# A two-block transformer stack on one core: one matmul of 512 columns for the high weights, and token-major blocks of 512

## The chip, the cores and the metric

The kernel runs on one core of a Trainium2 chip. The time is that of the device, in microseconds, of one execution of the whole program; less is better.

## The reference

Two blocks of two layers each work on 256 tokens of 1024 features, in float32. Cut to what matters here:

```
def first_block(...):                                # two layers
    h = h + 0.5 * swiglu(rms_norm(h, g1), w_in, w_out)        # 1024 -> 2 x 2816 -> 1024
    u = rms_norm(h, g); split(u @ w_in)                        # 11312 columns
    merged = sigmoid(gate_s) * (mamba2(...) @ w_s) + sigmoid(gate_d) * (deltanet(...) @ w_d)
    h = h + merged @ w_out
    h = h + 0.5 * swiglu(rms_norm(h, g2), w_in2, w_out2)
def second_block(...):                               # two layers
    u = rms_norm(h, g); q, k, v, g_ret, c_in, gates = split(u @ w_in)   # 10240 columns
    y_a = (silu(g_ret) * group_norm(chunk_retention(rot(q), rot(k), v))) @ w_ret_out
    y_b = silu(layer_norm(dwconv31(a * sigmoid(b)))) @ w_conv_out + bias
    h = h + (g_a * y_a + g_b * y_b) @ w_mix_out
    h = h + cross_attention(rms_norm(h), rms_norm(mem)) @ w_xo
    h = h + (silu(dwconv3(gate)) * val) @ w_down               # 1024 -> 2 x 2816 -> 1024
```

Almost all of the arithmetic is in the weight products.

## The kernel before

The residual stream `h` lies in SBUF as four tiles of 128 features x (2 feature tiles x 256 tokens). All weights are streamed once from HBM, in parts of [128 x 1024] (512 KB), 938 of them. `wpart` (L182) loads a part by DMA into `wr`, ScalarE casts it to `wh` (fp32r, the high part, L187), VectorE subtracts to get `wl` (the low part, L189). Each of these has four buffers. The activations are split in the same way, into tiles of high parts and tiles of low parts (class `X`, L192), each tile with two feature tiles of 256 tokens side by side. A product is then three matmuls of 256 columns: high weights by high x, high weights by low x, low weights by high x.

`proj_fm` (L202) makes two tiles of 128 output features in one PSUM bank `pw`: for each of the two and for each 128 rows of the contraction it issues the three matmuls, with the weights stationary and 256 tokens moving:

```
TE.matmul(o, a, x.h(k), start=(k == 0), stop=False)
TE.matmul(o, a, x.l(k), start=False, stop=False)
TE.matmul(o, b, x.h(k), start=False, stop=(k == KT - 1))
```

With a contraction of 1024 such a unit takes two weight parts and 48 matmuls. `proj_tm` (L219) makes the products that are wanted with tokens on partitions (`zd`, `zs`, `v`, `g` and the values of the cross attention): x is stationary there and 256 columns of the weights move, again three matmuls, for two token tiles, in one bank.

`ffn` (L331) and `conv_ffn` (L1103) loop over eleven pairs of a gate and an up unit, and then call `out_proj` (L326), four units with a contraction of 2816. In front of the product x carries the gain of the norm only; the reciprocal root mean square (`rb`) is multiplied in where the accumulator is evacuated, since it is not ready when the stream begins. `mixer1` (L399) holds the delta rule and the state space branch, `mixer2` (L830) the retention (`rot` L914, `by_tokens` L922) and the convolution branch of 31 taps (L902), `xattn` (L1048) the cross attention.

What sets the order: the stream has the highest priority (`AHEAD`), and `tick()` (L161) lets the other work, written as generators ("chains"), go one step after each part of a unit; the convolution's taps are dealt out by `PUMP` = 3.1 per part, each behind the subtraction that was issued last. A scheduler places instructions on each engine by these priorities. PSUM has eight banks: four single-bank buffers of `pw` for the stream, four of `pm` for everything else.

Of the kernel before, what the change touches and what calls it, by code (L numbers as in the profile page):

```python
# [15 lines left out]
P = 128  # L16
# [8 lines left out]
AHEAD = 100000  # priority of what the weight stream needs  # L25
PUMP = 3.1  # convolution taps dealt out per unit of the weight stream

# per-feature vectors, one column of 128 features each: name -> columns per layer
# [25 lines left out]
# column ranges of w_in, in the order in which they are streamed  # L54
# [15 lines left out]
W1F, W1T = _starts(W1_FM, 128), _starts(W1_TM, 256)  # L70
W2F, W2T = _starts(W2_FM, 128), _starts(W2_TM, 256)


def _kernel(tc, t):
    nc = tc.nc
    V, A, G, TE = nc.vector, nc.scalar, nc.gpsimd, nc.tensor
    with ExitStack() as es:
# [22 lines left out]

        def pw():
            return pwp.tile([P, 512], F32, name="pw")
# [51 lines left out]
        def split(hi, lo, src):  # L154
            A.copy(hi, src)
            sub(lo, src, hi.bitcast(F32))

# [34 lines left out]
        class X:  # L192
            def __init__(self):
                self.hi, self.lo = [], []

            def h(self, k):
                return self.hi[k // 2][:, (k % 2) * 256:(k % 2) * 256 + 256]

            def l(self, k):
                return self.lo[k // 2][:, (k % 2) * 256:(k % 2) * 256 + 256]  # L200

        def proj_fm(w, i, KT, x):  # L202
            """tiles i, i+1 of w (features on partitions): one bank [128, (2, 256 tokens)]"""
            p = pw()
            for m in range(2):
                o = p[:, m * 256:m * 256 + 256]
                for k0 in range(0, KT, 8):
                    kt = min(8, KT - k0)
                    hi, lo = wpart(w[i + m, :, k0 * 128:(k0 + kt) * 128], kt * 128)
                    for kk in range(kt):  # L210
                        k = k0 + kk
                        a, b = hi[:, kk * 128:kk * 128 + 128], lo[:, kk * 128:kk * 128 + 128]
                        TE.matmul(o, a, x.h(k), start=(k == 0), stop=False)  # L213
                        TE.matmul(o, a, x.l(k), start=False, stop=False)  # L214
                        TE.matmul(o, b, x.h(k), start=False, stop=(k == KT - 1))  # L215
                    tick()
            return p

        def proj_tm(w, i, x):  # L219
            """block i (256 columns) of w, tokens on partitions: one bank [128, (2 token tiles, 256)]"""  # L220
            parts = [wpart(w[i, :, q * 1024:(q + 1) * 1024], 1024) for q in range(2)]
            p = pw()
            for tk in range(2):
                o = p[:, tk * 256:tk * 256 + 256]
                s = slice(tk * 128, tk * 128 + 128)
                for k in range(8):
                    hi, lo = parts[k // 4]
                    a, b = hi[:, (k % 4) * 256:(k % 4) * 256 + 256], lo[:, (k % 4) * 256:(k % 4) * 256 + 256]
                    TE.matmul(o, x.h(k)[:, s], a, start=(k == 0), stop=False)  # L229
                    TE.matmul(o, x.l(k)[:, s], a, start=False, stop=False)  # L230
                    TE.matmul(o, x.h(k)[:, s], b, start=False, stop=(k == 7))  # L231
                tick()
            return p

# [1 line left out]
        class Norm:  # L236
            def __init__(self, g, alloc=None):
                self.g, self.x, self.acc = g, X(), None
                self.alloc = alloc
# [5 lines left out]
            def operand(self, j, h):  # L245
                if self.alloc is None:
                    hi = xp.tile([P, 512], F32R, name="xh")
                    lo = xp.tile([P, 512], F32R, name="xl")
                else:
                    hi, lo = self.alloc(F32R), self.alloc(F32R)  # L250
                for m in range(2):
                    k = 2 * j + m
                    s = slice(m * 256, m * 256 + 256)
                    A.activation(hi[:, s], h[:, s], AF.Copy, scale=self.g[:, k:k + 1])
                    V.scalar_tensor_tensor(lo[:, s], h[:, s], self.g[:, k:k + 1], hi[:, s].bitcast(F32), op0=ALU.mult, op1=ALU.subtract)
                self.x.hi.append(hi)
                self.x.lo.append(lo)
# [8 lines left out]
            def scaled(self, h):  # L266
                """the normalized operand itself"""
                y = X()
                for j in range(4):
# [4 lines left out]
                    hi, lo = xp.tile([P, 512], F32R, name="xh"), xp.tile([P, 512], F32R, name="xl")  # L274
                    split(hi, lo, v)
                    y.hi.append(hi)
                    y.lo.append(lo)
# [18 lines left out]
        def total(acc):  # L296
            """sums over features of a tile of feature pairs: a bank's [128 tokens, 2 token tiles]"""
# [6 lines left out]
        def rows(col, name):  # L304
            """[128 tokens, 2] -> [128, 256 tokens], the same on each partition"""
# [25 lines left out]
        def ffn(h, L, nrm, w1, w2, nxt):  # L331
# [3 lines left out]
            for j in range(NF // 2):  # L335
                pg = proj_fm(w1[L], 2 * j, 8, x)
                pu = proj_fm(w1[L], NF + 2 * j, 8, x)
                g, u = cv(), cv()
                mul(r2(g), r2(pg), rbb)
                A.activation(g, g, AF.Silu)  # L340
                mul(r2(u), r2(pu), rbb)
                mul(g, g, u)
                hi, lo = sa(F32R), sa(F32R)
                split(hi, lo, g)
                hid.hi.append(hi)
                hid.lo.append(lo)

            def evac(j, p):
                V.scalar_tensor_tensor(h[j], p, 0.5, h[j], op0=ALU.mult, op1=ALU.add)
# [4 lines left out]
        def conv_silu(p, rb, w, K, nt, c0, bias, dst):  # L354
            """causal depthwise convolution of two tiles (p times rb, or p alone), then silu"""
# [18 lines left out]
        def fm(tiles, i, c):  # L374
            """feature tile i, chunk (or token tile) c"""
# [8 lines left out]
        def to_features(tm, u, g, dst):  # L384
            """two feature tiles 2u, 2u+1 of tm (by tokens), times the gains g, as hi and lo"""
# [4 lines left out]
            hi, lo = sa(F32R), sa(F32R)  # L390
            n = 512 // g.shape[1]
            for m in range(g.shape[1]):
                s = slice(m * n, m * n + n)
                A.activation(hi[:, s], p[:, s], AF.Copy, scale=g[:, m:m + 1])
                V.scalar_tensor_tensor(lo[:, s], p[:, s], g[:, m:m + 1], hi[:, s].bitcast(F32), op0=ALU.mult, op1=ALU.subtract)
            dst.hi.append(hi)
            dst.lo.append(lo)

        def mixer1(h, L, nrm, nxt):  # L399
# [4 lines left out]
            # small projections: dt (32), a (8), b (8)  # L404
# [18 lines left out]
            # softplus(x) = max(x, 0) + log1p(exp(-|x|)), log1p(e) = 2 atanh(e / (2 + e))  # L423
# [18 lines left out]
            # cumulated decays: by column (tokens on partitions), totals, by row (through DRAM)  # L442
# [16 lines left out]
            def fetch(r0, c):  # L459
                """rows r0..r0+3 of the cumulated decays, chunk c, on each partition"""  # L460
# [5 lines left out]
            def decays(dst, r0, c):  # L466
                """fetched rows to exp(min(row - column, 0)): [column token, (4, row token)]"""
# [5 lines left out]
            # -- gated delta rule, four heads at a time: chunks of 128, unnormalized k and q, their norms folded into the scalings --  # L473
# [7 lines left out]
            def ssq(tiles):  # L481
                """rsqrt of the sums of squares over features: columns (chunk, head)"""
# [14 lines left out]
            def delta(hh, kf, qf, vf, zd):  # L497
# [6 lines left out]
                # M[i, j] = c1[i] exp(G_i - G_j) k_i k_j (its lower part counts); a[j, i] = exp(G_i - G_j) q_i k_j for j <= i  # L504
# [21 lines left out]
                # Y = transposed inverse of I + M, by doubling the diagonal blocks; Z = its transpose (32-column windows)  # L526
# [15 lines left out]
                def aside():  # L542
                    """what the inverse does not need: k by tokens, scaled for the state (chunk 0) and for w (chunk 1); a; v; scales of q"""
# [14 lines left out]
                for lvl in range(1, 6):  # L558
                    # rows of the upper blocks: (off-diagonal block of the transposed M) times Y, then Y times that
# [114 lines left out]
            def tm_silu(dst, i, u):  # L674
                p = proj_tm(wt, i + u, state1["x"])
# [637 lines left out]
```

## Time and profile before

| | us |
|---|---|
| median of 3 runs | 2968.93 |
| lowest and highest run | 2967.71, 2970.07 |
| span of the profiled execution (first to last instruction) | 2968.0 |
| TensorE busy | 2950.8 (99%) |
| VectorE busy | 2202.5 (74%) |
| ScalarE busy | 1526.6 (51%) |

The time of the profiled execution is its span and the little that lies around it; the three runs are within 0.1% of each other. Busy times are sums of records of an engine; the records of matmuls overlap, so a busy TensorE says that it always had one under way. Where an engine was idle, the views name what ended the idle time. A window is a stretch of the span, counted from its first instruction.

### The profile page before, as it was taken

To read this page: it belongs to the slowest core of one execution; us is meant where nothing else is said; L and a number is where in the kernel's file an instruction comes from. 1 tells how busy PE (TensorE), PEld (TensorE's weight loads), DVE (VectorE), ACT (ScalarE), POOL (GpSimd) and SP (SyncE) were. 2 spreads that over 40 slices of the span, in tenths; PEclk is the share of its full clock that TensorE was granted. 3 is DMA by queue.
4 is the path that set the end of the run, shared out by engine and by line. 5 is a ranking of instruction groups with operands and counts; after the bars stand their busy time and mean duration, and the time that the engine had idled before them with its cause. 6 is when DMAs were issued, how large, how long until landed. Compare 5 with 4: busy or idle time off the path is not lost.

```text
span 2968.0 us, 62381 instructions
## 1 busy us (share of the span) xinstructions
PE 2950.8 (99%) x26256; PEld 2911.2 (98%) x26256; DVE 2202.5 (74%) x3498; ACT 1526.6 (51%) x2080; POOL 95.0 (3%) x113
## 2 busy tenths in 40 slices
PE   8999999999999999999999999999999999999998
PEld 8999999999999999999999999999999999999998
DVE  6658878866666578788665799976676899876774
ACT  5446456544444465465454544545554444554553
POOL 0000001100000001011000000000000000000000
PEclk9999999999999999999999999999999999999999
DMA  6555444455655555444556555555456554554554
GB/s 229 180 172 185 144 136 136 161 181 185 180 183 183 175 171 165 129 142 154 173 189 194 175 172 169 171 176 166 157 185 192 185 166 161 178 177 151 171 181 132
DMA packets 141690, 505.51 MB, mean 170 GB/s; under 512 B 16164, under 2 KB 16550, under 8 KB 141408
## 3 DMA queue, kind: packets, MB, share of 16 engines
q1 hardware_dynamic: 137808, 490.29, 51.5%
q0 software_dynamic: 3312, 10.70, 1.3%
q8 instruction: 205, 3.36, 0.5%
q14 instruction: 77, 0.63, 0.1%
q10 hardware_dynamic: 288, 0.52, 0.0%
HBM read 500.32 MB, written 1.13 MB: 169 GB/s over the span
## 4 chain that ended last, share of the span: by engine, by line
PE 99%; DVE 0%; ACT 0%; issue 0%; DMA 0%; POOLq 0%; DVEq 0%; SPq 0%; ACTq 0%
PE pw L213 26%; PE pw L215 26%; PE pw L214 26%; PE pw L229 4%; PE pw L230 4%; PE pw L231 4%; PE pm L742 1%; PE pm L389 1%; PE pm L566 0%; PE pm L1058 0%; PE pm L1084 0%; PE pm L580 0%; PE pm L961 0%; PE pm L551 0%; PE pm L603 0%; PE pm L310 0%
## 5 line engine op out<-in xcount | busy, mean ns | idle before, releaser
L187 ACT CAST wh<-wr 128x1024 fp32r<-128x1024 f32 (+1 forms) x938 | 969.3, 1036 | 1225.8 <-PE pw L214 866.9
L189 DVE TENSOR_TENSOR wl<-wr,wh 128x1024 fp32r<-128x1024 f32 (+1 forms) x938 | 1129.8, 1207 | 536.4 <-ACT wh L187 532.6
L213 PE MATMUL pw<-xh,wh 128*128 128x256 f32 x3712 | 1068.6, 288 | 7.6 <-ACT wh L187 7.6
L214 PE MATMUL pw<-xl,wh 128*128 128x256 f32 x3712 | 1057.3, 285 | 0.0
L215 PE MATMUL pw<-xh,wl 128*128 128x256 f32 x3712 | 1055.7, 285 | 0.7 <-DVE wl L189 0.7
L213 PE MATMUL pw<-sa,wh 128*128 128x256 f32 x2656 | 752.1, 284 | 0.7 <-DVE sa L137 0.7
L214 PE MATMUL pw<-sa,wh 128*128 128x256 f32 x2656 | 752.6, 284 | 0.0
L215 PE MATMUL pw<-sa,wl 128*128 128x256 f32 x2656 | 751.3, 283 | 0.0
L213 PEld LDWEIGHTS pw<-xh,wh 128*128 128x128 f32 x3712 | 717.0, 193 | 12.9 <-ACT wh L187 9.6
L214 PEld LDWEIGHTS pw<-xl,wh 128*128 128x128 f32 x3712 | 717.6, 193 | 4.9 <-issue 4.8
L215 PEld LDWEIGHTS pw<-xh,wl 128*128 128x128 f32 x3712 | 717.0, 193 | 1.9 <-DVE wl L189 1.3
L214 PEld LDWEIGHTS pw<-sa,wh 128*128 128x128 f32 x2656 | 509.8, 192 | 0.6 <-issue 0.5
L213 PEld LDWEIGHTS pw<-sa,wh 128*128 128x128 f32 x2656 | 509.2, 192 | 1.0 <-issue 0.9
L215 PEld LDWEIGHTS pw<-sa,wl 128*128 128x128 f32 x2656 | 509.5, 192 | 0.5 <-issue 0.5
L229 PE MATMUL pw<-wh,xh 128*128 128x256 f32 x832 | 238.8, 287 | 0.0
L231 PE MATMUL pw<-wl,xh 128*128 128x256 f32 x832 | 236.7, 285 | 0.0
L230 PE MATMUL pw<-wh,xl 128*128 128x256 f32 x832 | 235.8, 283 | 0.0
L902 DVE SCALAR_TENSOR_TENSOR sb<-sa,dw,sb 128x237 f32<-128x237 f32 (+20 forms) x480 | 201.9, 461 | 0.0
L229 PEld LDWEIGHTS pw<-wh,xh 128*128 128x128 f32 x832 | 159.5, 192 | 0.6 <-issue 0.5
L230 PEld LDWEIGHTS pw<-wh,xl 128*128 128x128 f32 x832 | 159.5, 192 | 0.5 <-issue 0.5
L231 PEld LDWEIGHTS pw<-wl,xh 128*128 128x128 f32 x832 | 159.4, 192 | 0.0
L137 DVE TENSOR_TENSOR cv<-pw,rb 128x512 f32<-128x512 f32 x118 | 81.2, 691 | 64.3 <-PE pw L215 62.2
(310 smaller groups left out, 2500.1 us busy)
## 6 DMA issues: line engine op xcount, KB each, us to landing
wr<-in_w1f_dram SPq DMA_DIRECT2D x128, 512.0 KB, 3.4
wr<-in_w2f_dram SPq DMA_DIRECT2D x96, 512.0 KB, 3.3
wr<-in_f1i_dram SPq DMA_DIRECT2D x88, 512.0 KB, 3.4
wr<-in_f2i_dram SPq DMA_DIRECT2D x88, 512.0 KB, 3.3
wr<-in_wup_dram SPq DMA_DIRECT2D x88, 512.0 KB, 3.3
wr<-in_w2t_dram SPq DMA_DIRECT2D x64, 512.0 KB, 4.3
wr<-in_w1t_dram SPq DMA_DIRECT2D x48, 512.0 KB, 3.8
wr<-in_f1o_dram SPq DMA_DIRECT2D x32, 512.0 KB, 3.5
```

What stands on the lines that cost most here:

```text
L137: V.tensor_tensor(out, a, b, op=ALU.mult)
L187: A.copy(hi[:, :n], r[:, :n])
L189: last[0] = V.tensor_tensor(lo[:, :n], r[:, :n], hi[:, :n].bitcast(F32), op=ALU.subtract)
L213: TE.matmul(o, a, x.h(k), start=(k == 0), stop=False)
L214: TE.matmul(o, a, x.l(k), start=False, stop=False)
L215: TE.matmul(o, b, x.h(k), start=False, stop=(k == KT - 1))
L229: TE.matmul(o, x.h(k)[:, s], a, start=(k == 0), stop=False)
L230: TE.matmul(o, x.l(k)[:, s], a, start=False, stop=False)
L231: TE.matmul(o, x.h(k)[:, s], b, start=False, stop=(k == 7))
L389: TE.transpose(p[:, m * 256 + c * 128:m * 256 + c * 128 + 128], tm[c][:, (2 * u + m) * 128:(2 * u + m) * 128 + 128], ident)
L742: TE.matmul(p[:, i * 64:i * 64 + 64], mt[i // 4][:, (i % 4) * 128:(i % 4) * 128 + 128], xdt[:, i * 64:i * 64 + 64], start=True, stop=True)
L902: V.scalar_tensor_tensor(om[:, tap:], xm[:, :256 - tap], wc, om[:, tap:], op0=ALU.mult, op1=ALU.add)
```

## The change

`X` now keeps, for each feature tile, the high and the low part of 256 tokens side by side in one tile of 512 columns, `t[k]`. With `wide=True`, `proj_fm` issues per 128 rows of the contraction one matmul of 512 columns, high weights by `t[k]`, and one of 256, low weights by the high part. The products with high x and with low x then lie in two halves of a bank, and a unit takes two banks. The evacuation adds the halves: `gather` copies one half on ScalarE and adds the other on VectorE; the output projections that end in `h` add both halves to it, in two instructions. All output projections are wide, and the pairs of the feed forwards from the third on (`EARLY` = 2): for these the normalized operand itself is made by `scaled`, `rb` included, after the first pair. `proj_tm` now makes blocks of 512 columns: x stationary, 512 weight columns moving, two token tiles in two banks, each weight part used as it comes; the host lays these weights out in blocks of 512. `pw` has two buffers of two banks where it had four of one. `xp` has eight tiles of one feature tile each. Splits are done per feature tile, so in halves.

```diff
-        hp, xp = pool("hp", 4), pool("xp", 4)
+        hp, xp = pool("hp", 4), pool("xp", 8)
-        pwp = es.enter_context(tc.tile_pool(name="pw", bufs=4, space=bass.MemoryType.PSUM))
+        pwp = es.enter_context(tc.tile_pool(name="pw", bufs=2, space=bass.MemoryType.PSUM))
...
-            return pwp.tile([P, 512], F32, name="pw")
+            return pwp.tile([P, 1024], F32, name="pw")
...
+            def add(self, src):
+                for m in range(src.shape[1] // 256):
+                    s = src[:, m * 256:m * 256 + 256]
+                    hi, lo = self.new()
+                    A.copy(hi, s)
+                    sub(lo, s, hi.bitcast(F32))
...
+                o = p[:, m * 512:m * 512 + 512] if wide else p[:, m * 256:m * 256 + 256]
...
+                        if wide:
+                            if k:
+                                TE.matmul(o[:, :256], b, x.h(k), start=False, stop=False)
+                            TE.matmul(o, a, x.t[k], start=(k == 0), stop=(k == KT - 1))
+                            if k == 0:
+                                TE.matmul(o[:, :256], b, x.h(k), start=False, stop=False)
...
+        def parts(p):
+            v = p.rearrange("p (m s t) -> p m s t", m=2, s=2)
+            return v[:, :, 0, :], v[:, :, 1, :]
+        def gather(dst, p):
+            a, b = parts(p)
+            A.copy(r2(dst), b)
+            add(r2(dst), a, r2(dst))
...
-            parts = [wpart(w[i, :, q * 1024:(q + 1) * 1024], 1024) for q in range(2)]
+            p = [p[:, :512], p[:, 512:]]
+            for q in range(4):
+                hi, lo = wpart(w[i, :, q * 1024:(q + 1) * 1024], 1024)
+                for kk in range(2):
+                    k = 2 * q + kk
+                    a, b = hi[:, kk * 512:kk * 512 + 512], lo[:, kk * 512:kk * 512 + 512]
+                    for tk in range(2):
+                        s = slice(tk * 128, tk * 128 + 128)
+                        TE.matmul(p[tk], x.h(k)[:, s], a, start=(k == 0), stop=False)
+                        TE.matmul(p[tk], x.l(k)[:, s], a, start=False, stop=False)
+                        TE.matmul(p[tk], x.h(k)[:, s], b, start=False, stop=(k == 7))
...
-                evac(j, proj_fm(w, 2 * j, KT, x))
+                evac(j, proj_fm(w, 2 * j, KT, x, wide=True))
...
+                wide = j >= EARLY
+                pg = proj_fm(w1[L], 2 * j, 8, x, wide)
+                pu = proj_fm(w1[L], NF + 2 * j, 8, x, wide)
                 g, u = cv(), cv()
+                if wide:
+                    gather(g, pg)
+                    A.activation(g, g, AF.Silu)
+                    gather(u, pu)
...
+                if j == EARLY - 2:
+                    xs = nrm.scaled(h, sa)
+                if j == EARLY - 1:
+                    x = xs
                 mul(g, g, u)
+                hid.add(g)
             def evac(j, p):
-                V.scalar_tensor_tensor(h[j], p, 0.5, h[j], op0=ALU.mult, op1=ALU.add)
+                for part in parts(p):
+                    V.scalar_tensor_tensor(r2(h[j]), part, 0.5, r2(h[j]), op0=ALU.mult, op1=ALU.add)
```

In the order of instructions on TensorE, the first feed forward before (the names are output<-x, weights):

```order
L213 MATMUL pw<-xh,wh 128x256
L214 MATMUL pw<-xl,wh 128x256
L215 MATMUL pw<-xh,wl 128x256
L213 MATMUL pw<-xh,wh 128x256
L214 MATMUL pw<-xl,wh 128x256
L215 MATMUL pw<-xh,wl 128x256
```

and after the change, in the same stage, at the end of one tile of 128 features and the beginning of the next:

```order
L241 MATMUL pw<-sa,wh 128x512
L240 MATMUL pw<-sa,wl 128x256
L241 MATMUL pw<-sa,wh 128x512
L240 MATMUL pw<-sa,wl 128x256
L241 MATMUL pw<-sa,wh 128x512 x2
L243 MATMUL pw<-sa,wl 128x256
L240 MATMUL pw<-sa,wl 128x256
L241 MATMUL pw<-sa,wh 128x512
```

Three instructions per 128 rows have become two, one of them of 512 columns; over the program 19,104 + 3,072 matmuls of the two projections have become 3,936 of 512 and 3,936 of 256 in wide units, 7,296 of 256 in the others, and 1,536 of 512 in `proj_tm`.

On VectorE, in `mixer2` of the first layer, before: the q unit `pw_21784` is evacuated by the products with `cs` (cosine and sine), between taps (`sb<-sa,dw,sb`) and low parts (`wl`):

```order
L318 TENSOR_SCALAR ms_21913<-mv_21909 128x1
L944 SCALAR_TENSOR_TENSOR fac2_21857<-mv_21854,fac2_21857 128x1
L902 SCALAR_TENSOR_TENSOR sb_20885<-sa_20882,dw_20755,sb_20885 128x231 x2
L902 SCALAR_TENSOR_TENSOR sb_21026<-sa_21023,dw_20755,sb_21026 128x243
L189 TENSOR_TENSOR wl_22106<-wr_22102,wh_22104 128x1024
L902 SCALAR_TENSOR_TENSOR sb_21026<-sa_21023,dw_20755,sb_21026 128x243
L137 TENSOR_TENSOR st_21865<-pw_21784,cs_20708 128x512
L137 TENSOR_TENSOR st_21866<-pw_21784,cs_20708 128x512
L902 SCALAR_TENSOR_TENSOR sb_20885<-sa_20882,dw_20755,sb_20885 128x230
```

and after the change, where the q unit is `pw_19134`, the k unit takes the parts `wl_19226` and `wl_19274`, and the v unit, which takes the accumulator of q next, the parts from `wl_19316` to `wl_19380`:

```order
L930 SCALAR_TENSOR_TENSOR sb_18329<-sa_18326,dw_18199,sb_18329 128x227
L190 TENSOR_TENSOR wl_19380<-wr_19376,wh_19378 128x1024
L930 SCALAR_TENSOR_TENSOR sb_18329<-sa_18326,dw_18199,sb_18329 128x226
L930 SCALAR_TENSOR_TENSOR sb_18470<-sa_18467,dw_18199,sb_18470 128x244
L971 SCALAR_TENSOR_TENSOR fac2_19207<-mv_19204,fac2_19207 128x1
L930 SCALAR_TENSOR_TENSOR sb_18470<-sa_18467,dw_18199,sb_18470 128x243
L346 TENSOR_SCALAR ms_19263<-mv_19259 128x1
L930 SCALAR_TENSOR_TENSOR sb_18329<-sa_18326,dw_18199,sb_18329 128x226
L930 SCALAR_TENSOR_TENSOR sb_18470<-sa_18467,dw_18199,sb_18470 128x243
L141 TENSOR_TENSOR st_19215<-pw_19134,cs_18152 128x512
L141 TENSOR_TENSOR st_19216<-pw_19134,cs_18152 128x512
```

The evacuation stands behind the fourth part of the v unit (the rows of one column between belong to the group norm of the head before). Before, a unit's bank was used again by the fourth unit after it; now it is used again by the second.

## Rows read from the trace of the kernel before

**Rows 1.** The page: span; busy time of each engine; granted TensorE clock in 40 slices.
```profile
span 2968.0 us, 62381 instructions
PE 2950.8 (99%) x26256; PEld 2911.2 (98%) x26256; DVE 2202.5 (74%) x3498; ACT 1526.6 (51%) x2080; POOL 95.0 (3%) x113
PEclk9999999999999999999999999999999999999999
```

**Rows 2.** The page: the chain that ended last, share of the span by engine.
```profile
PE 99%; DVE 0%; ACT 0%; issue 0%; DMA 0%; POOLq 0%; DVEq 0%; SPq 0%; ACTq 0%
```

**Rows 3.** Groups of TensorE by line and form (busy us, mean ns | idle before).
```profile
L213 PE MATMUL pw<-xh,wh 128*128 128x256 f32 x3712 | 1068.6, 288 | 7.6 <-ACT wh L187 7.6
L213 PE MATMUL pw<-sa,wh 128*128 128x256 f32 x2656 | 752.1, 284 | 0.7 <-DVE sa L137 0.7
L229 PE MATMUL pw<-wh,xh 128*128 128x256 f32 x832 | 238.8, 287 | 0.0
L229 PE MATMUL pw<-wh,sa 128*128 128x256 f32 x192 | 54.7, 285 | 0.0
```

**Rows 4.** Timeline of TensorE in the first feed forward (start, duration, us).
```profile
99.83 0.28 PE L213 MATMUL pw<-xh,wh 128*128 128x256 f32 x1
...
100.19 0.28 PE L213 MATMUL pw<-xh,wh 128*128 128x256 f32 x1
```

**Rows 5.** Windows (us: span, PE, PEld, DVE, ACT, POOL busy; clock; DMA share; GB/s).
```profile
649.00:840.00 191.00, 191.00 (x1595) 191.00 (x1594) 118.03 (x131) 88.97 (x104) 0.70 (x1) 1.00 0.58 182
1668.00:2042.00 374.00, 373.30 (x3043) 366.62 (x3042) 328.54 (x589) 187.01 (x270) 9.25 (x12) 1.00 0.53 172
355.00:356.40 1.40, 1.40 (x9) 1.40 (x8) 1.37 (x5) 0.00 (x0) 0.30 (x1) 0.50 0.01 3
```

**Rows 6.** Timeline of TensorE in that stretch at half clock.
```profile
355.08 0.41 PE L213 MATMUL pw<-xh,wh 128*128 128x256 f32 x1
...
355.72 0.41 PE L213 MATMUL pw<-xh,wh 128*128 128x256 f32 x1
```

**Rows 7.** Timeline of TensorE, 48 weight columns.
```profile
215.18 0.28 PE L409 MATMUL pm<-sa,wh 128*48 128x256 f32 x1
...
215.77 0.28 PE L411 MATMUL pm<-sa,wl 128*48 128x256 f32 x1
```

**Rows 8.** Timeline of TensorE, float32 products of 128 and of 256 columns.
```profile
1274.48 0.60 PE L389 MATMUL pm<-ident,st 128*128 128x128 f32 x4
...
2057.78 1.89 PE L1058 MATMUL pm<-sa 128*128 128x256 f32 x8
```

**Rows 9.** Groups of TensorE by form: the same two lines.
```profile
L389 PE MATMUL pm<-ident,st 128*128 128x128 f32 x32 | 5.4, 272 | 0.0
L1058 PE MATMUL pm<-sa 128*128 128x256 f32 x64 | 15.8, 379 | 0.0
```

**Rows 10.** Groups of VectorE and ScalarE by line.
```profile
L189 DVE TENSOR_TENSOR wl<-wr,wh 128x1024 fp32r<-128x1024 f32 (+1 forms) x938 | 1129.8, 1207 | 536.4 <-ACT wh L187 532.6
L902 DVE SCALAR_TENSOR_TENSOR sb<-sa,dw,sb 128x237 f32<-128x237 f32 (+20 forms) x480 | 201.9, 461 | 0.0
L349 DVE SCALAR_TENSOR_TENSOR h<-pw,h 128x512 f32<-128x512 f32 x16 | 11.1, 692 | 5.5 <-PE pw L215 5.5
L273 DVE SCALAR_TENSOR_TENSOR st<-h,v,rb 128x256 f32<-128x256 f32 x24 | 10.1, 471 | 0.0
L140 DVE TENSOR_TENSOR st<-st 128x256 f32<-128x256 f32 x20 | 8.4, 422 | 0.4
L143 DVE TENSOR_TENSOR sa<-cv,sa 128x512 fp32r<-128x512 f32 x44 | 30.1, 685 | 0.0
L683 ACT ACTIVATE sb<-pw 128x512 f32<-128x512 f32 x16 | 9.5, 592 | 0.0
```

**Rows 11.** Timelines, mixer2: last matmul of a q unit, and its evacuation.
```profile
1755.53 0.28 PE L215 MATMUL pw<-xh,wl 128*128 128x256 f32 x1
...
1770.97 1.28 DVE L137 TENSOR_TENSOR st<-pw,cs 128x512 f32<-128x512 f32 x2
```

More of the change, by code (lines that the diff above doesn't have):

```diff
@@ L25 @@
 AHEAD = 100000
+EARLY = 2
 PUMP = 3.1
@@ L219, in proj_tm @@
+                    tick()
+            return p if wide else p[:, :512]
+        def parts(p):
[5 more added lines that the diff above has]
+            add(r2(dst), a, r2(dst))
         def proj_tm(w, i, x):
-            parts = [wpart(w[i, :, q * 1024:(q + 1) * 1024], 1024) for q in range(2)]
             p = pw()
[L223 to L231, printed above, removed]
+            p = [p[:, :512], p[:, 512:]]
[9 more added lines that the diff above has]
+                        TE.matmul(p[tk], x.h(k)[:, s], b, start=False, stop=(k == 7))
@@ L245, in operand @@
             def operand(self, j, h):
[L246 to L257, printed above, removed]
+                self.x.add_scaled(h, self.g[:, 2 * j:2 * j + 2])
             def square(self, h):
@@ L273, in scaled @@
                         V.scalar_tensor_tensor(v[:, s], h[j][:, s], self.g[:, 2 * j + m:2 * j + m + 1], self.rb, op0=ALU.mult, op1=ALU.mult)
[L274 to L277, printed above, removed]
+                    y.add(v)
                 return y
@@ L923, in by_tokens @@
                 dst = [sa(), sa()]
-                for u in range(2):
-                    p = proj_tm(wt, i + u, xs)
-                    for tk in range(2):
-                        A.activation(dst[tk][:, u * 256:u * 256 + 256], p[:, tk * 256:tk * 256 + 256], func)
+                p = proj_tm(wt, i, xs)
+                for tk in range(2):
+                    A.activation(dst[tk], p[tk], func)
                 return dst
@@ L1011, in evac @@
             def evac(j, p):
-                V.scalar_tensor_tensor(h[j], p, 0.5, h[j], op0=ALU.mult, op1=ALU.add)
+                for part in parts(p):
+                    V.scalar_tensor_tensor(r2(h[j]), part, 0.5, r2(h[j]), op0=ALU.mult, op1=ALU.add)
                 nxt.feed(j, h[j])
@@ L1094, in xattn @@
                 start(head(hd, q))
-            mem.values(range(1, 4))
+            mem.values(range(1, 2))
             drain()
             def evac(j, p):
-                add(h[j], p, h[j])
+                for part in parts(p):
+                    add(r2(h[j]), part, r2(h[j]))
                 nxt.feed(j, h[j])
@@ L1108, in conv_ffn @@
             for j in range(NF // 2):
-                pg = proj_fm(t["wup"][L], NF + 2 * j, 8, x)
-                pv = proj_fm(t["wup"][L], 2 * j, 8, x)
+                wide = j >= EARLY
+                pg = proj_fm(t["wup"][L], NF + 2 * j, 8, x, wide)
+                pv = proj_fm(t["wup"][L], 2 * j, 8, x, wide)
                 o, u = st(), st()
-                conv_silu(pg, rb, w, 3, NF, 2 * j, bias, o)
-                mul(r2(u), r2(pv), rbb)
+                if wide:
+                    cx = cv()
+                    gather(cx, pg)
+                    conv_silu(cx, None, w, 3, NF, 2 * j, bias, o)
+                    gather(u, pv)
+                else:
+                    conv_silu(pg, rb, w, 3, NF, 2 * j, bias, o)
+                    mul(r2(u), r2(pv), rbb)
+                if j == EARLY - 2:
+                    xs = nrm.scaled(h, sa)
+                if j == EARLY - 1:
+                    x = xs
                 mul(o, o, u)
-                hi, lo = sa(F32R), sa(F32R)
-                split(hi, lo, o)
-                hid.hi.append(hi)
-                hid.lo.append(lo)
+                hid.add(o)
             def evac(j, p):
-                add(h[j], p, h[j])
+                for part in parts(p):
+                    add(r2(h[j]), part, r2(h[j]))
                 nxt.feed(j, h[j])
```

141 lines of the change are left out of this document (66 added, 75 removed).

## The prediction

> **What bounds the kernel now.** I read the engine table first: TensorE is busy 2950.8 us of a span of 2968.0, VectorE 74%, ScalarE 51%, at full clock nearly throughout [rows 1]. The chain of waits says the same: 99% of what ended last is TensorE, and nothing that it waits for has a share of even 1% [rows 2]. So a microsecond more or less of TensorE is a microsecond of the kernel, and other engines count only where TensorE begins to wait for them. The groups of instructions show what fills it: the three lines of `proj_fm` run 3712 + 2656 times each and those of `proj_tm` 832 + 192 times each, 22,176 stream matmuls of 256 columns in all [rows 3]. A record's own duration (284 to 288 ns) is no price, since records overlap; the pitch from start to start is. In a feed forward the starts stand 120 ns apart, three steps in 0.36 us [rows 4]. 22,176 x 0.120 = 2661 us; the other 307 us are the float32 products, the start and the end, which the change leaves alone.
>
> **What a matmul of 512 columns costs** appears in no row, and the forecast hangs on it. 256 columns at 2.4 GHz are 106.7 ns, so the 120 hold 13.3 ns that are not columns. Three rows speak of what these are.
> - Where the granted clock is 0.50 (1.2 GHz, third row of [rows 5]), three steps take 0.64 us, 213 ns each [rows 6]: 256 / 1.2 = 213.3, nothing added. So whatever makes the 13.3 ns hides under a record whose columns take long, or is no issue at half the rate.
> - With 48 weight columns in place of 128, five steps take 0.59 us [rows 7], 118 ns each. The weight load alone does not make it.
> - Float32 products with 128 columns pass twice through the array, 106.7 ns too, with the same weight load: four records in 0.60 us, one of them 272 ns long, are (600 - 272) / 3 = 109 ns apart [rows 8, 9]. Eight of 256 columns, 379 ns long each, take 1.89 us: (1890 - 379) / 7 = 216 ns, against 213.3 of columns [rows 8, 9]. These lose 2 to 3 ns per record.
>
> So the surcharge belongs to reading 256 new fp32r columns in 107 ns, and is not in the weights. If it arises once per instruction, 512 columns take 213.3 + 13.3 = 226.7 ns; if it arises per column, 240; if it disappears in a record as long as the float32 ones, 216. 216 and 240 are the ends of my range. I take 226.7: it is the middle, and the second row of [rows 8] and [rows 6] show that a record with over 200 ns of array time need not carry a part that grows with it, while the first says that fp32r does cost more than float32 for equal array time.
>
> **The change part by part.**
> - Removed: per wide step of the contraction one `a` matmul. From the order of instructions, 3936 of the 6368 steps become wide: 464 in each of the six feed forwards (the pairs from the third on and the down projection), 256 in each of four mixers, 64 in each cross attention. Each does 512 + 256 columns in two instructions where it did 3 x 256. The token-major blocks have 1536 matmuls of 512 where 3072 of 256 stood. Together 3936 + 1536 = 5472 instructions fewer, and the columns are the same. At 240 - 226.7 = 13.3 ns each: **-73 us**; at the ends 0 and 5472 x 24 = -131 us. Per feed forward, 464 x 13.3 = 6.2 of 191.0 us [rows 5].
> - Weights: the same 938 parts of 512 KB or less, the same casts and subtractions, the same order on SP's queue. A part of eight wide steps lasts 8 x (226.7 + 120) = 2.77 us instead of 2.88; VectorE's 1.21 us per part [rows 10] fit beside it. Nothing.
> - VectorE, added: 48 evacuations of output projections in two passes of 0.69 us, +33; 32 gathered additions before a product of gates, +22; six calls of `scaled`, each 8 x 0.47 + 8 x 0.42 = 7.1, +43; the halves of `add(src)`, 2 x 0.42 for 0.69, 114 times, +18 [rows 10]. About 116 us, to 2319 of some 2920: 79%. It lies beside TensorE where VectorE has room: 118 of 191 us in a feed forward, and only just in mixer2 (328.5 of 374.0 before, [rows 5]; about 340 of 364 after, with 12 x 0.69 and the halves). Its cost is in the next item.
> - ScalarE, added: 132 gathering copies at 0.59 us [rows 10], +78 us to 1526.6, and some 50 more for the casts by halves and the six calls (an estimate from half of the same row). Half of its time is free: nothing, except in the next item.
> - **Buffers.** Four accumulators `pw` become two. A unit of 48 matmuls lasts 5.76 us, so before, a reader could be 17 us late and nobody waited; now it has one unit. In mixer2 the q unit ended at 1755.81 is read at 1770.97, 15.2 us later, because taps of the convolution stand ahead on VectorE [rows 11]. In the new order of VectorE I looked for evacuations that stand behind the fourth low part from the beginning of the next-but-one unit. That part's `wl` buffer, one of four, comes free only when the unit between is consumed, so TensorE has then nothing left to do but that next-but-one unit, and waits for the evacuation. There are nine such places: two q units, one product of the convolution branch, two `dnw` gathers, two queries of the cross attention, two starts of the conv feed forward. The rows of VectorE's order after the change show one q place: behind the part `wl_19380` stand five taps at 0.46, two of a single column, and the evacuation of 1.28 [rows 10, 11], about 4 us. The other eight have 2 to 5 us by the same count; nine x 3 = **+27 us**. Behind the waiting matmul the whole TensorE queue stands, and the weight parts after it; the stream's four parts of lead refill while it stands, so nothing else is late. Feed-forward starts and places with a slack under one part: another +3. Below, nothing is lost if VectorE runs ahead; above, 15.2 - 5.8 = 9.4 us at each of nine places, 85.
> - `proj_tm` now takes four parts in the order of arrival, not two at once: fewer parts are held back. Nothing, as TensorE never waited there.
>
> Sum: 2968.0 - 73 + 30 = 2925 us for the profiled execution; the median of the three runs is 0.9 above its span, so **2926**.
>
> One rule of the Trainium skill bears on this. The float32 row of 216 ns [rows 8] carries about 2.5 ns per record, the fp32r rows 13.3. The Trainium skill, "TensorE: Matmul & The Clock Gate", section "Wait — 56ns, not 53.3ns?", states a fixed cost of about 2.5 ns per matmul that shows only at the full clock, and 215.7 ns for 512 columns. The trace agrees for float32 and at half clock, and disagrees for 256 columns of fp32r (120, not 109). By its 215.7 ns the first term would be 5472 x 24.3 = -133 us, an estimate, which is the gain of the third rival; if only its fixed 2.5 ns were saved, 5472 x 2.5 = -14 us.
>
> **The rivals.**
> - *The surcharge is per column* (slower). 512 columns take 240 ns, as two of 256 do, and the first term is 0; what is left is the buffers: 2968 + 30, **2998**. For it: the first row of [rows 8] has equal array time and weights with half the columns read, and no surcharge; at half the column rate there is none either [rows 6]. Against it: no float32 row shows a part that grows with the columns. It decides from a pitch above 234.5 ns, where 5472 x 5.5 = 30. Chance 0.24.
> - *Two accumulators eat it.* The pitch falls to 227, but at the nine places TensorE waits the whole lateness that the old trace shows, 9.4 us: -73 + 85, **2980**. For it: VectorE in mixer2 is at 88% already. Against: in feed forwards it is at 62% [rows 5]. From 8 us per place on, nothing is gained. Chance 0.10.
> - *The surcharge disappears in long records.* 216 ns as in float32: -131 + 30, **2868**. For it: the rows of 216 and of 213 at half clock; against: in those the columns are read at half the rate. Chance 0.16.
> - That the change does not do what it says is excluded by the order of instructions, which has the 512-column matmuls in all the places named.
>
> **How the numbers follow.** The forecast has 0.50: 2926, give or take 25 (waits of 5 to 55 us), so 2901 to 2951. The range of 2862 to 2995 takes in the third rival, the second, and the upper part between; it leaves out most of the worse half of the first rival and waits beyond the bounds, under 2 in 10. A measurement tells about 0.2% or 6 us from no change. Faster: 0.50 + 0.16, and a fraction of the second rival, 0.67. Same: 0.09, where 235 ns meets 30 us of waits, or the second rival's waits are near 73. Slower: 0.24.
>
> **What would show it.** The pitch in the wide stretch of a feed forward: alternating 512 and 256 starts should be 227 and 120 ns apart, sum 347; 336 means the third rival, 360 the first. A feed forward should take 185 us in place of 191. The token-major line should have the same pitch. VectorE busy should be near 2319 us, ScalarE near 1650. The idle time before `pw` matmuls should name VectorE's multiplications by `cs` and `rb` as releasers, about 30 us in all, mostly in mixer2; the q place should show 4 us. If TensorE's idle time exceeds 60 us, or the granted clock falls in the wide stretches, I am wrong in a way that the sum does not hold.

## The result and the profile after

The changed kernel takes 3009.35 us (median of 4 runs, 3008.95 to 3010.31) against 2969.39 for the kernel before: a ratio of 1.0136, 95% interval 1.0124 to 1.0148, so **slower by 40 us** where 43 faster was forecast. The span of its profiled execution is 3006.9 us against 2968.0, +38.9.

The page of the changed kernel: span, busy times, TensorE's granted clock in 40 slices, the chain by engine.

```profile
span 3006.9 us, 52196 instructions
...
PE 2927.2 (97%) x20784; PEld 2630.7 (87%) x20784; DVE 2291.3 (76%) x3796; ACT 1616.4 (54%) x2318; POOL 96.9 (3%) x113
PEclk9999999999999999999999999999999999999999
...
PE 93%; DVE 4%; ACT 2%; issue 1%; DMA 0%; SPq 0%; POOLq 0%; ACTq 0%; DVEq 0%
```

Against [rows 1, 2]: TensorE works 23.6 us less, but the span is longer, so it stands still 79.7 us where it stood 17.2; VectorE and ScalarE, with under 1% of the chain before, hold 6% of it. Summed over the gaps between the records of TensorE, without the ends, its idle time is 68 us; it was 2. The mean granted clock (lists of the cores, before and after) has fallen too:

```profile
core 0: 2968.0 us, clock 0.995
...
core 0: 3006.9 us, clock 0.987
```

Time at half clock is 2 x (1 - clock) x span: 78 us against 30. Half of that is lost, 39 against 15, or a little less, as 5 us of it lie inside the waits themselves.

What the matmuls cost now, in a feed forward and in a token-major block (timelines of TensorE: start, duration in us):

```profile
99.14 0.40 PE L241 MATMUL pw<-sa,wh 128*128 128x512 f32 x1
99.38 0.28 PE L240 MATMUL pw<-sa,wl 128*128 128x256 f32 x1
...
100.20 0.40 PE L241 MATMUL pw<-sa,wh 128*128 128x512 f32 x1
...
1794.67 0.39 PE L273 MATMUL pw<-wh,xt 128*128 128x512 f32 x1
...
1796.03 0.39 PE L273 MATMUL pw<-wh,xt 128*128 128x512 f32 x1
```

From 99.14 to 100.20 lie three pairs of 512 and 256: 353 ns a pair, where three matmuls of 256 took 360 [rows 4]. From 1794.67 to 1796.03 lie six of 512 columns: 227 ns each, where two of 256 took 240. Over all such steps of the trace at the full clock the means are 351 and 228. So the columns give 3936 x 9 = 35 us in the wide units and 1536 x 12 = 18 in the token-major blocks, **-53 us** together.

The whole difference is then: -53 for the instructions, +66 idle time (68 - 2), +24 half clock (39 - 15) = +37, against 38.9 measured between the spans.

Where TensorE waits, longest sums first (engine and line, whom it waited for: us in all, times, longest; the wait for the first weights at the start, 7.7 us, stands in the row of L188 and is there in the kernel before too):

```profile
PE pw L272 <- DVE st L141: 13.4, 4, 6.3
PE pw L245 <- ACT wh L188: 9.8, 3, 7.7
PE pw L241 <- DVE st L144: 8.8, 4, 3.5
PE pm L1103 <- DVE cv L1098: 6.7, 4, 2.8
PE pw L241 <- DVE cv L144: 6.0, 2, 3.0
PE pw L245 <- DVE cv L141: 5.8, 6, 1.0
PE pw L245 <- DVE cv L403: 4.9, 4, 2.2
```

All but the second and the fourth are an accumulator that VectorE has not yet read out. One of the two longest waits, 5.6 us, stands at the q unit of [rows 11] (timelines of TensorE and VectorE; the other, 6.3 us, is that of the second layer):

```profile
1777.56 0.28 PE L247 MATMUL pw<-xt,wl 128*128 128x256 f32 x1
1783.41 0.77 PE L272 MATMUL pw<-wh,xt 128*128 128x512 f32 x1 [5.58 <-DVE st L141]
...
1778.83 1.23 DVE L190 TENSOR_TENSOR wl<-wr,wh 128x1024 fp32r<-128x1024 f32 x1
...
1781.98 1.29 DVE L141 TENSOR_TENSOR st<-pw,cs 128x512 f32<-128x512 f32 x2
```

The k unit ends at 1777.84, the fourth low part of the v unit is begun at 1778.83, and behind it come taps and small rows, as the order showed; the v unit starts when the product with `cs` is done. And it then starts at half clock. The windows (columns as in [rows 5]): a feed forward and mixer2 after the change; mixer2 and mixer1 before it; mixer1 after it; and, after it, the stretch around this wait in three parts:

```profile
654.40:843.80 189.40, 187.13 (x1129) 165.67 (x1128) 126.54 (x165) 100.57 (x141) 0.70 (x1) 1.00 0.60 183
1674.40:2064.50 390.10, 378.64 (x2417) 341.05 (x2416) 342.48 (x617) 195.37 (x274) 9.22 (x12) 0.99 0.55 168
...
1666.20:2042.00 375.80, 375.10 (x3058) 368.42 (x3057) 330.07 (x591) 188.77 (x272) 9.25 (x12) 1.00 0.53 172
203.20:649.00 445.80, 445.79 (x4676) 434.87 (x4676) 351.75 (x655) 254.72 (x372) 35.91 (x38) 0.98 0.48 156
...
199.60:654.40 454.80, 446.66 (x4132) 409.05 (x4131) 359.38 (x677) 260.57 (x380) 35.79 (x38) 0.97 0.50 153
...
1777.80:1782.50 4.70, 0.04 (x1) 0.00 (x0) 4.70 (x13) 1.78 (x2) 1.32 (x2) 1.00 0.38 120
1782.50:1789.30 6.80, 5.88 (x14) 4.66 (x15) 6.80 (x18) 1.55 (x2) 0.00 (x0) 0.50 0.05 22
1789.30:1794.00 4.70, 4.70 (x22) 3.84 (x22) 3.88 (x8) 1.33 (x2) 0.00 (x0) 1.00 0.39 111
```

The granted clock falls to 0.50 at 1782.5, towards the end of the 5.6 us without a matmul, and is back at 1.00 at 1789.3: 5.9 us of matmuls run at half clock. The Trainium skill, "TensorE: Matmul & The Clock Gate", section "Part 1: The HAM clock gate (the "warmup" mystery)", says that an array which has stood idle falls back to half its clock and gets the full one only after it has been busy again; these windows agree. Ten such stretches, 44 us together, stand at ten of the eleven waits of 2.2 us or more; at the waits of about 1 us, but for those at the very end, there is none. The other 33 us of half clock, as the 30 of the kernel before, lie in mixer1, behind small products without any wait, and at the end.

The feed forward gains 1.6 us of the forecast 6.2. Mixer2 takes 14 us more than before (the window of [rows 5] begins 15 matmuls later than the one shown here), 5 of them for the block of values that has moved there: 24 matmuls at 227 ns. Mixer1, where the prediction had two of its nine places, takes 9 more. Over all stages the four feed forwards gain 10 us together; the two mixer1 lose 18, mixer2 and the cross attention 23, the conv feed forwards 7.

### The profile page after: what moved, and what is told of

It reads as the page before. It is cut to its first block, busy times and chain, and to the rows that moved or that the text cites. A ratio compares the mean times of both kernels' runs of the same rounds, so it can differ in the third digit from the quotient of the medians.

```text
span 3006.9 us, 52196 instructions
## 1 busy us (share of the span) xinstructions
PE 2927.2 (97%) x20784; PEld 2630.7 (87%) x20784; DVE 2291.3 (76%) x3796; ACT 1616.4 (54%) x2318; POOL 96.9 (3%) x113
## 4 chain that ended last, share of the span: by engine, by line
PE 93%; DVE 4%; ACT 2%; issue 1%; DMA 0%; SPq 0%; POOLq 0%; ACTq 0%; DVEq 0%
PE pw L241 30%; PE pw L240 14%; PE pw L245 9%; PE pw L246 9%; PE pw L247 9%; PE pw L272 4%; PE pw L274 4%; PE pw L273 4%; PE pw L243 1%; DVE wl L190 1%; PE pm L770 1%; PE pm L425 1%; ACT wh L188 1%; DVE cv L403 0%; PE pm L595 0%
## 5 line engine op out<-in xcount | busy, mean ns | idle before, releaser
L188 ACT CAST wh<-wr 128x1024 fp32r<-128x1024 f32 (+1 forms) x938 | 971.1, 1037 | 1136.7 <-PE pw L241 375.6
L241 PE MATMUL pw<-sa,wh 128*128 128x512 f32 x3936 | 1366.5, 399 | 14.8 <-DVE st L144 8.8
L240 PE MATMUL pw<-sa,wl 128*128 128x256 f32 x3560 | 998.6, 281 | 0.0
L241 PEld LDWEIGHTS pw<-sa,wh 128*128 128x128 f32 x3936 | 716.7, 189 | 162.3 <-DVE st L144 10.0
L245 PE MATMUL pw<-xt,wh 128*128 128x256 f32 x1984 | 579.1, 293 | 25.8 <-ACT wh L188 9.8
L247 PE MATMUL pw<-xt,wl 128*128 128x256 f32 x1984 | 567.9, 286 | 0.7 <-DVE wl L190 0.7
L246 PE MATMUL pw<-xt,wh 128*128 128x256 f32 x1984 | 567.3, 286 | 0.0
L245 PEld LDWEIGHTS pw<-xt,wh 128*128 128x128 f32 x1984 | 384.3, 194 | 34.1 <-issue 11.2
L246 PEld LDWEIGHTS pw<-xt,wh 128*128 128x128 f32 x1984 | 385.0, 194 | 5.2 <-issue 4.3
L247 PEld LDWEIGHTS pw<-xt,wl 128*128 128x128 f32 x1984 | 384.6, 194 | 2.7 <-issue 1.4
L272 PE MATMUL pw<-wh,xt 128*128 128x512 f32 x416 | 171.8, 413 | 15.1 <-DVE st L141 13.4
L274 PE MATMUL pw<-wl,xt 128*128 128x512 f32 x416 | 167.0, 402 | 0.0
L273 PE MATMUL pw<-wh,xt 128*128 128x512 f32 x416 | 166.3, 400 | 0.0
L245 PE MATMUL pw<-sa,wh 128*128 128x256 f32 x448 | 127.1, 285 | 2.3 <-DVE sa L916 1.2
L247 PE MATMUL pw<-sa,wl 128*128 128x256 f32 x448 | 127.4, 285 | 0.0
L246 PE MATMUL pw<-sa,wh 128*128 128x256 f32 x448 | 127.0, 284 | 0.0
L243 PE MATMUL pw<-sa,wl 128*128 128x256 f32 x376 | 105.1, 280 | 0.0
L403 DVE SCALAR_TENSOR_TENSOR cv<-pw,v,cv 128x255 f32<-128x255 f32 (+2 forms) x240 | 102.6, 472 | 0.1
```

Source lines behind the costliest of these rows:

```text
L188: A.copy(hi[:, :n], r[:, :n])
L240: TE.matmul(o[:, :256], b, x.h(k), start=False, stop=False)
L241: TE.matmul(o, a, x.t[k], start=(k == 0), stop=(k == KT - 1))
L243: TE.matmul(o[:, :256], b, x.h(k), start=False, stop=False)
L272: TE.matmul(p[tk], x.h(k)[:, s], a, start=(k == 0), stop=False)
L273: TE.matmul(p[tk], x.l(k)[:, s], a, start=False, stop=False)
```

## The experiments

The theories. **A**: the accumulators. Two of two banks, where four of one stood, make TensorE wait for evacuations, and the clock falls behind the waits. **B**: the added work on VectorE (second additions, gathering, splits by halves, `scaled`) makes the waits. P, Q and M are about single points. Idle time is always the sum of the gaps between TensorE's records (2 us before, 68 after); ratios are to the kernel before, with 95% intervals.

**Two accumulators in the old kernel.**

```diff
-        pwp = es.enter_context(tc.tile_pool(name="pw", bufs=4, space=bass.MemoryType.PSUM))
+        pwp = es.enter_context(tc.tile_pool(name="pw", bufs=2, space=bass.MemoryType.PSUM))
```

> The kernel before with one edit: two accumulators pw of one bank each in place of four. No matmul, no addition and no split is changed. Theory A (the changed kernel lost by waiting for two accumulators, and by the half clock that follows such a wait): TensorE's idle time rises from 2 us to between 30 and 70 us, the mean granted clock falls from 0.995 to 0.985 to 0.991, the time is 3010 to 3060 us. Theory B (two accumulators are enough for the old kernel, and the waits of the changed kernel come from the additions, splits and calls of scaled that VectorE got): within 10 us of 2969.

Measured: 3014.8 us, 1.0156 (1.0141 to 1.0171); idle 39 us. Its clock, its busy times and its waits for accumulators:

```profile
core 0: 3011.4 us, clock 0.993
...
PE 2960.0 (98%) x26256; PEld 2916.2 (97%) x26256; DVE 2205.3 (73%) x3498; ACT 1527.6 (51%) x2076; POOL 96.2 (3%) x113
...
PE pw L213 <- ACT sb L677: 6.9, 4, 3.0
PE pw L229 <- DVE fac L944: 6.7, 1, 6.7
PE pw L213 <- DVE cv L137: 5.7, 6, 1.0
PE pw L229 <- DVE st L137: 4.9, 1, 4.9
```

Not one instruction was added, VectorE is as busy as before, and the kernel is 45 us slower: as much as by the whole change. The two long waits before L229 are those of the two q units, 4.9 and 6.7 us (5.6 and 6.3 in the changed kernel); the second is put down to `fac`, a product of one column just behind the one with `cs`, which ends 0.1 us before. The idle time is in the range of theory A, the clock a little better than in it. B falls as the main cause. Of the 90 us of idle time and half clock, though, this accounts for half.

**Four accumulators of one bank in the changed kernel.**

```diff
-        pwp = es.enter_context(tc.tile_pool(name="pw", bufs=2, space=bass.MemoryType.PSUM))
+        pwp = es.enter_context(tc.tile_pool(name="pw", bufs=4, space=bass.MemoryType.PSUM))
-            return pwp.tile([P, 1024], F32, name="pw")
+            return pwp.tile([P, 512], F32, name="pw")
...
             for m in range(2):
+                if wide:
+                    p.append(pw())
+                    o = p[m]
...
```

> The changed kernel with four accumulators of one bank: a wide unit or a token-major block takes two of them, a narrow unit one, as before the change. The additions into h and the gathering are done per bank, in instructions of 256 columns, so VectorE and ScalarE get more of them. Theory A: the waits at the q units, the convolution product and the queries, where narrow units follow each other, go; those of the dnw gathers and the starts of the wide pairs stay; idle 20 to 40 us in place of 68, clock 0.990 or more, time 2945 to 2975. Theory B (VectorE's added work makes the waits): idle 60 us or more, time 3000 to 3030.

Measured: 2974.8 us, 1.0016 (1.0007 to 1.0026); idle 46 us, clock 0.991. The time is at the upper end of theory A, and 35 us of the loss are back; but the idle time is over A's range. The waits at the q units and the convolution product are gone. A new one has come, 7.4 us in each mixer2, in its first output projection:

```profile
1936.54 0.60 PE L353 MATMUL pm<-dg,cst 128*128 128x128 f32 x4
1944.53 0.77 PE L245 MATMUL pw<-sa,wh 128*128 128x512 f32 x1 [7.38 <-DVE st L144]
```

A wide unit takes two single accumulators, so wide units in a row have the depth of two again, and here VectorE is late with the additions of the gathering, behind the layer norm of the convolution branch. So B has a share where wide units follow each other next to a loaded VectorE.

**The eight matmuls of 512 of a weight part first, then the eight of 256.**

```diff
-                            if k:
-                                TE.matmul(o[:, :256], b, x.h(k), start=False, stop=False)
-                            TE.matmul(o, a, x.t[k], start=(k == 0), stop=(k == KT - 1))
...
+                            for kk in range(g0, min(kt, g0 + G)):
+                                k = k0 + kk
+                                TE.matmul(o, ab(kk)[0], x.t[k], start=(k == 0), stop=False)
+                            for kk in range(g0, min(kt, g0 + G)):
+                                k = k0 + kk
+                                TE.matmul(o[:, :256], ab(kk)[1], x.h(k), start=False, stop=(k == KT - 1))
```

> The changed kernel with the wide matmuls of a weight part in another order: all eight of 512 columns, then all eight of 256. Theory P (a 512 next to a 256 costs 231 to 241 ns because the two alternate, the weight load of the one hiding badly under the other): starts 227 ns apart as in the token-major blocks, 120 among the 256, 347 per step in place of 352; 3936 x 5 = 20 us less, 2985 to 2995. Theory Q (the 235 belong to the operand that moves, the x tiles, or to one accumulator written again and again): 233 or more among the 512 too, and a time within 8 us of 3009, or more if the 256 stay at 120.

Measured: 3014.3 us, 1.0151 (1.0135 to 1.0168). The groups in a feed forward (timeline of TensorE):

```profile
700.50 1.11 PE L245 MATMUL pw<-sa,wl 128*128 128x256 f32 x8
701.45 2.00 PE L242 MATMUL pw<-sa,wh 128*128 128x512 f32 x8
```

With the last record's 0.28 and 0.40 us taken off, the starts are 119 and 229 ns apart. The single starts show more: the first two 512s behind the 256s are 235 ns from their successors in the mean, the last three 227. So P is right in that a run of 512s settles at 227, and wrong in the gain: the 256s among themselves go back from 117 to 120, and the step costs 349 in place of 351. The idle time is 75 us, and the time is within 8 us of the changed kernel's, as Q said. Nothing is to be had from this order.

**Only the token-major blocks, in single banks** (all units narrow, no `scaled` in the feed forwards).

```diff
-EARLY = 2
+EARLY = 99
...
-                evac(j, proj_fm(w, 2 * j, KT, x, wide=True))
+                evac(j, proj_fm(w, 2 * j, KT, x))
...
```

> The changed kernel with four accumulators of one bank and no wide unit at all: only the token-major blocks of 512 columns are left of the change, with the splits by halves. 1536 matmuls at 228 in place of 3072 at 120: -18 us. Theory A: almost no idle time (under 10 us), clock as before, 2949 to 2957. Theory B: the blocks of 512 bring waits of their own (they take two accumulators at once): idle 20 us or more, 2965 or more.

Measured: 2974.6 us, 1.0017 (1.0008 to 1.0027); idle 19 us. My expectation A failed. The time is B's, with an idle time just under B's 20 us, but not for B's reason. The token-major pitch is 228, as expected; 9.2 of the 19 us are one wait of the softmax chain, twice in each cross attention:

```profile
PE pm L1113 <- DVE cv L1108: 9.2, 4, 2.8
```

**The values of the cross attention in blocks of 256 again.** Before, one block of 256 columns ran in mixer2 and three in the cross attention; in blocks of 512 it is one and one, so the cross attention has a quarter of the values' matmuls less beside its softmax chain.

```diff
-                    p = proj_tm(t["wxv"][self.L], u, self.n.x)
...
+                    p = proj_tm1(t["wxv"][self.L], u, self.n.x)
...
-            mem.values(range(1, 2))
+            mem.values(range(1, 4))
...
```

> As the kernel with token-major blocks of 512 in single banks and no wide unit (2974.6 us), but the values of the cross attention in blocks of 256, one of them in mixer2 and three in the cross attention, as before the change. Theory M (the blocks of 512 moved one of three value blocks' work out of the cross attention, and its softmax chain lost that cover: 5.2 us idle in each cross attention, and half clock after the second): idle falls from 19 us to 7 or 9, 2958 to 2966. If the chain waits for another reason, the idle time in the cross attention stays at 5 us and the time at 2972 or more.

Measured: 2962.4 us, 0.9976 (0.9967 to 0.9986); idle 8.5 us. The window of the second cross attention before this edit (in the kernel above), and then with it:

```profile
2688.60:2771.30 82.70, 77.50 (x523) 71.93 (x522) 47.46 (x75) 36.87 (x56) 0.69 (x1) 0.96 0.42 127
```

```profile
2679.50:2759.20 79.70, 79.70 (x618) 77.89 (x617) 49.84 (x77) 40.20 (x62) 0.70 (x1) 1.00 0.45 146
```

(`proj_tm1` makes blocks of 256 columns.) More matmuls, less time: the cover had been taken away. Theory M holds, and the same wait (L1103) cost the changed kernel 6.7 us.

**The changed kernel without wide units, with its two accumulators of two banks.** (The edit of `EARLY` and `wide` above, with the `pw` of the change.)

> The changed kernel without any wide unit (so without the gathering, the second additions into h and the calls of scaled in the feed forwards), but with its two accumulators of two banks and its token-major blocks of 512. Theory A (the accumulators cost what they cost in the old kernel, 45 us, and the token-major blocks give 18): 2990 to 3000, idle time 35 to 50 us. Theory B (the waits come mainly with the wide units): 2955 to 2970, idle under 25 us.

Measured: 3016.6 us, 1.0161 (1.0144 to 1.0178); idle 50 us, clock 0.991. It is slower than either theory said; theory A had not counted the cover lost in the cross attention (12 us, above). Beside the kernel with the same blocks in four single banks (2974.6), from which it differs in the accumulators alone, it is 42 us slower: they cost here about what they cost in the old kernel. And the wide units, over the whole of the changed kernel (3009 with them), gave 7 us of the 35 that their pitch is worth.

**Wide feed forwards only, in single banks, token-major blocks of 256.**

```diff
-                evac(j, proj_fm(w, 2 * j, KT, x, wide=True))
+                evac(j, proj_fm(w, 2 * j, KT, x, wide=KT == NF))
...
+EARLYC = 4
...
-                wide = j >= EARLY
+                wide = j >= EARLYC
...
```

> Four accumulators of one bank; wide units only in the six feed forwards (pairs from the third on, in the conv feed forwards from the fifth on, and their down projections), each taking two accumulators; the output projections of the mixers and of the cross attention narrow, the token-major blocks of 256 as before the change. Theory A: 9 ns per wide step as measured in the feed forwards with single banks (191.0 to 186.8), 2656 steps, -24 us, and almost no wait: 2942 to 2950, idle under 12 us, clock as before. Theory B (the wide unit's added work on VectorE brings waits also there): 2955 or more.

Measured: 2943.6 us, 0.9914 (0.9899 to 0.9928); idle 2.6 us, clock 0.996. Theory A, within its range.

**The same with token-major blocks of 512 in mixer2.**

> As the kernel with wide feed forwards only, and in mixer2 the token-major blocks of 512 columns, taking two of the four accumulators. 768 matmuls at 227 in place of 1536 at 120: -9 to -10 us more, 2933 to 2941. If the blocks bring waits in mixer2, where VectorE is at 88%: idle 8 us more or above, and no gain over the kernel without them.

Measured: **2936.5 us**, 0.9889 (0.9874 to 0.9904), idle 4.7 us. Within what I had expected, and faster than both kernels. Its busy times, a feed forward and mixer2:

```profile
PE 2914.6 (99%) x22832; PEld 2723.7 (93%) x22832; DVE 2272.1 (77%) x3888; ACT 1602.9 (55%) x2418; POOL 106.2 (4%) x113
...
643.60:830.00 186.40, 186.40 (x1130) 165.51 (x1129) 128.23 (x188) 101.58 (x160) 0.70 (x1) 1.00 0.61 186
1648.70:2020.70 372.00, 370.39 (x2674) 348.10 (x2673) 331.01 (x603) 189.61 (x267) 12.10 (x12) 1.00 0.55 173
```

VectorE has 70 us more to do than before [rows 1], and a feed forward takes 186.4 in place of 191.0 [rows 5] without a gap: its added work is hidden there.

**Four more wide output projections** (those that end in `h`, and the one behind the convolution branch).

```diff
-                evac(j, proj_fm(w, 2 * j, KT, x, wide=KT == NF))
+                evac(j, proj_fm(w, 2 * j, KT, x, wide=KT != 16 and evac.__name__ != "evac_d"))
```

> As the fastest kernel so far (wide feed forwards in single banks, token-major blocks of 512 in mixer2, 2936.5 us), with four more output projections per pair of layers wide: those that end in h, and the one behind the convolution branch; 512 more steps. Theory A (a wide step gives 9 ns where no wait comes with it): -4 to -5 us, 2931 to 2934. If their evacuations, now two additions per bank on VectorE, come late for two accumulators: idle 5 us more or above, 2937 to 2950.

Measured: 2936.5 us, 0.9890 (0.9876 to 0.9905): no difference, so neither expectation. Each mixer2 is 1.4 us shorter, the cross attentions are 2 and 3 us longer, with waits of 0.9 us for the additions into `h` and, behind one of them, 3.4 us at half clock. Gain and loss cancel. So four of the seven output projections outside the feed forwards cost nothing by being wide. What the other three (those that are gathered before a product of gates), mixer1's blocks of 512 and the earlier wide pairs of the conv feed forwards cost the changed kernel, no run took apart.

## Why the prediction was wrong

- *TensorE bounds the kernel, and only its waits let others in.* Right; the chain and the gaps tell the whole difference.
- *512 columns cost 226.7 ns, the surcharge being one per instruction.* Right for matmuls of 512 in a row: 227. The per-column rival (240) is excluded, and so is 216. The Trainium skill's 215.7 ns ("TensorE: Matmul & The Clock Gate", section "Wait — 56ns, not 53.3ns?") is not reached by fp32r here in any row: the least pitch is 223. Where 512 and 256 alternate, the pair costs 351, not 347, and this I had not in the sum: it took 13.3 ns for each step, where 360 - 351 leaves 9 and 240 - 228 leaves 12. The first term was -53, not -73. Why the alternation costs 4 ns is open; grouping by eight does not change it much. What the prediction said of float32 rests on 109 and 216 ns alone: that these products pass twice through the array no row shows, and the weight loads of those with 128 columns take 140 ns, not 193 as in the stream, so they are not "the same".
- *VectorE's added work.* 2291 us measured, 2319 forecast (ScalarE 1616, near 1650). By itself it is hidden in the feed forwards, as the 186.4 us show; it has a share where wide output projections stand beside a loaded VectorE.
- *Nine places, 27 us.* The nine came to 26: the q units 5.6 and 6.3, the `dnw` gathers 3.5 each, the first wide units of the conv feed forwards 3.0 each, the convolution product 1.2, the queries nothing; that the sum fits is partly luck, as single places miss by up to 3 us. But *"another +3"* for all the rest failed, **the largest miss of the sum**: the rest is about 40 us. It is the starts of the other units (L141, L144, L403, some 20 waits of about 1 us), the lost cover in the cross attention (5 us in each), and the end. I had counted only where VectorE's order forces a wait, not where an evacuation is merely later than the one unit that was left.
- *"so nothing else is late"*: a wait was priced at its length alone. **This step had no term at all for the clock.** A wait of some us costs its length and then the half clock: 48 us more at half clock, some 24 us lost. I had read the half-clock stretches [rows 5] for the pitch alone; those of the kernel before stand behind no wait, so they could not have shown it. With the short waits this makes the buffers' +30 into +90, and the sign that the prediction named for being wrong, more than 60 us of idle time, came (68).
- The rival that two accumulators eat the gain was the right one, at 0.10, and its price came close by luck: it was worked out from nine places at their whole lateness (85 us), where these nine gave 26 and the 90 come from many waits and the clock behind the longer ones. The edit that only halves the accumulators shows 45 us of it, and taking back the lost cover 12. If these add up, about 30 are left; the waits in the kernel with single banks put them down to wide units beside a loaded VectorE, but no run shows it.
- `proj_tm` at no cost failed too: its blocks of 512 moved work out of the cross attention that covered a softmax chain. Taking that back gave 12 us, in the kernel without wide units.

## What to carry to other kernels

When an edit fuses instructions and pays with buffers, run the old kernel with the fewer buffers alone: here that single number (+45 us) was as large as the whole result. Price a TensorE wait of some us at its length and the half clock behind it, and count every unit whose evacuation is later than the depth that is left, not only those that the order forces to wait. And allocate accumulators by the bank, so that only the units that need two take two: with that, and wide units only where VectorE has room, the same idea gave 2936.5 us, 1.1% under the kernel before.

## What the runs showed of the hardware

At the full clock fp32r matmuls in a row have a pitch of 120 ns with 256 columns and 227 with 512: 13 ns over their columns at 2.4 GHz both times. A 512 between two 256s starts 231 to 241 ns before its successor, and a run of 512s settles at 227 only after five. At a wait of 5.6 us the granted clock fell to 0.50, and the next 5.9 us of matmuls ran at it; at single waits of about 1 us it stayed at 1.00. In the kernel before it fell at 353.7 us without any idle time: 32 products of 32x32 and 16 of one column had filled the 2.4 us before.
